# A DiT kernel: seven block products in the first feed-forward too, modulation columns placed anew, and SyncE in program order

## The chip, the core and the metric

The kernel runs on one core of a Trainium2 chip. The metric is the device time of one execution in microseconds. A core has five engines that run their own instruction queues in order: PE (TensorE, matrix multiply, with its weight loads shown as PEld), DVE (VectorE), ACT (ScalarE), POOL (GpSimd) and SP (SyncE, which here issues nearly all loads from HBM). A queue stops at an instruction that waits for another engine's result, for a load, or for a buffer to come free.

## What is computed

A diffusion backbone of two layers on 512 latent tokens of width 1024, with 256 context tokens. Layer 0 mixes by Fourier heads and windowed attention, layer 1 by centred pooling. Each layer ends in a SwiGLU feed-forward with 2816 hidden channels. Every sub-layer has its own shift, scale and gate, which come from the conditioning vector. Cut to what matters here:

```python
def ada_mod(cond, w, b):
    m = jax.nn.silu(cond) @ w + b
    return jnp.split(m[..., None, :], 6, axis=-1)

def modulate(h, shift, scale):
    return h * (1 + scale) + shift

def swiglu(h, w1, w3, w2):
    return (jax.nn.silu(h @ w1) * (h @ w3)) @ w2
```

In each layer the feed-forward adds `gate * swiglu(modulate(rms_norm(h), shift, scale))` to `h`.

## The kernel before

**Layout and precision.** Activations lie with channels on the 128 partitions and the 512 tokens along the free dimension, so `h` is eight tiles of 128 x 512. A product in float32 is made of three passes: each operand is split into a high and a low part, and `passes` (L181 to L185) adds high by high (L183), low weight by high (L184) and high weight by low (L185). ACT makes a weight's high part `w_h` (L68), DVE the low part `w_l` (L153). The class `Stream` (L126) does this for all feed-forward weights: SP loads them into a ring of four raw buffers (`w_r`), ahead of their use.

**Stages.** The modulation of the first sub-layer, the input projections and the attention with its Fourier heads run to about 238 us. Then come layer 0's feed-forward (to 601), the pooling stage (to 638), layer 1's feed-forward (to 981), and the last norm with the stores.

**The feed-forward** (`ffn`, L1018) takes the 22 hidden tiles of 128 channels in groups of 8, 8 and 6 (`GROUPS`). After each group a down projection of eight steps (one for each tile of `h`, index `dt`) adds the group's part to `h` (L1083). Tile 0 is the lead tile (class `Lead`, L301): its product is taken from `h` before the norm's factor is known, and the shift's part, which is `wb` (DVE, L313 and L315) times ones (`sh_ps`, PE, L335), is added afterwards. Meanwhile `norm_apply` (L357) makes the normalized, modulated input of all other tiles: for each of eight channel tiles DVE writes `nrm_u` (L360), ACT `hnh` and DVE `hnl` (L366).

An ordinary tile multiplies two weights of 1024 rows by 512 tokens: 2 x 8 x 3 = 48 matmuls of 512 columns. In layer 1, tiles 4 to 21 (`QUARTERED`, L24) instead run as two by two blocks with seven block products in place of eight (class `Quarters`, L903): 7 x 4 x 3 = 84 matmuls of 256 columns. Sums of blocks of the input (`pieces`, L917: tiles `t_f`, `t_h`, `t_l`) are made once in the ordinary tiles before; sums of blocks of the weights (`prepare`, L944: `s_f`) for each tile. The low parts of the weights that are used as they are come by an accumulating transfer from POOL's queue (`low`, L937 to L942). The sums of blocks need `nrm_u`, so in layer 1 these eight tiles are kept, in the buffers of `a` (L1028, `NA` = 17).

**Modulation columns.** 80 of the columns of 128 modulation values are made one at a time by DVE (class `AdaCols`, L204): SP loads 512 KB into a raw buffer (`ada_r`, L215) and one DVE instruction multiplies by the conditioning vector and sums (L222). 24 are made in the attention (`acol`, over the units of `ADA`, L849: 2 in each of units 0 to 3, 4 in each of units 4 to 7), and 56 (`acol1`) in layer 0's tiles 2 to 21, three per tile (L1071 to L1073). The attention runs in eight such units; their columns are put on DVE in the place where the code stands (`pinned`).

**What sets the order.** In each queue a scheduler places the instructions, except where an engine is in `manual_schedule`, which keeps the order of the code: PE in layer 1's feed-forward. In the last down projection of layer 0, `pool_in` also prepares the pooling stage: it scales each finished tile of `h` (`pxh`, `pxl`, L355) and makes `wsh` (L1117, L1119); the norm adds squares (`sq`, L252).

Of the kernel before, what the change touches and what calls it, by code (L numbers as in the profile page):

```python
# [23 lines left out]
QUARTERED = (frozenset(), frozenset(range(4, NHID)))  # L24
NA = 17
# [6 lines left out]
def kernel(  # L32
# [93 lines left out]
    class Stream:  # L126
# [29 lines left out]
        def slots_for(self, n):  # L156
            pool, t = (wp_, "") if alt["pool"] is None or self.slots % 2 == 0 else (alt["pool"], "2")
            self.slots += 1
            return [pool.tile([P, n], F32R, tag=w + t, bufs=3, name=m) for w, m in (("whi", "w_h"), ("wlo", "w_l"))]

# [43 lines left out]
    class AdaCols:  # L204


        def __init__(self, blocks):
# [9 lines left out]
        def step(self, ahead=1):  # L217
# [4 lines left out]
            nc.vector.scalar_tensor_tensor(out=r, in0=r, scalar=1.0, in1=condB, op0=ALU.mult, op1=ALU.mult,  # L222
                                           accum_out=ada[l][:, t:t + 1])
# [170 lines left out]
    with ExitStack() as es:  # L394
# [507 lines left out]

    class Quarters:  # L903
# [79 lines left out]
        def run(self, left):  # L983
# [34 lines left out]
    def ffn(l, rstd, A, lead, each=None, pool=None):  # L1018
        nonlocal ss
        nrm = Norm(pf, T)  # L1020
# [15 lines left out]
        if quartered:  # L1036
            order.enter_context(tc.manual_schedule(engines={PE}))
        for gi, (j0, nj) in enumerate(GROUPS):
            a = []
            for j in range(j0, j0 + nj):  # L1040
# [269 lines left out]
```

## Time and profile before

| | us |
|---|---|
| median of 3 runs | 997.09 |
| the runs | 999.26, 995.76, 997.09 |
| profiled execution | 996.72 |
| its span, first to last instruction | 995.0 |
| mean granted TensorE clock | 0.994 |

The span is one execution as the hardware profiler recorded it; the profiled execution's own time is 1.7 us longer, as it includes what lies around the span. In the rows below, "L183" is line 183, `h_ps<-hnh,w_h` is the tile written and the tiles read, "x600" a count, and a group's numbers are its busy time in us, the mean of one in ns, and the idle time of the engine ahead of these instructions with what ended it.

```profile
L184 PE MATMUL h_ps<-hnh,w_l 128*128 128x512 f32 (+1 forms) x600 | 210.8, 351 | 0.4 <-DVE w_l L153 0.4
L183 PE MATMUL h_ps<-t_h,w_h 128*128 128x256 f32 x288 | 82.3, 286 | 1.4 <-DVE av L1060 0.9
L1083 DVE SCALAR_TENSOR_TENSOR h<-w_ps,ada,h 128x512 f32<-128x512 f32 x48 | 36.0, 750 | 91.2 <-PE w_ps L185 91.2
```

Matmuls overlap in the pipeline, so the time of one is longer than its share; the distance from one start to the next is what counts.

### The profile page before, as it was taken

Reading aid. Unit: us, or ns where it says so; the run is one execution under the profiler, and the core shown is the slowest. Engines: PE = TensorE matmul, PEld = TensorE weight load, DVE = VectorE, ACT = ScalarE, POOL = GpSimd, SP = SyncE. Lnnn points to the kernel's source line nnn. Section 1 sums busy time; section 2 is a strip of 40 time slices with the busy share of each in tenths; the row PEclk is TensorE's granted clock in tenths of the full one; section 3 lists DMA queues with packets and bytes.
Section 4 is the critical chain, followed back from the end, with each engine's and each line's share of the span. In section 5 each row is a group of like instructions: output and inputs, shape, how many; then the busy total and the mean of one; then the engine's idle time right before and its main releaser. Section 6 shows DMA issues by size and latency. Waiting matters only on the chain.

```text
span 995.0 us, 14007 instructions
## 1 busy us (share of the span) xinstructions
PE 962.3 (97%) x5464; PEld 804.6 (81%) x5464; DVE 665.6 (67%) x1086; ACT 450.6 (45%) x707; POOL 58.5 (6%) x63
## 2 busy tenths in 40 slices
PE   5999999998999999999999999999999999999995
PEld 3767777776888888888888888789988999889984
DVE  4678677879966546655365388998645776458644
ACT  4467666445632212223122365675533765337531
POOL 1011011002000000000000001000010110101100
PEclk9999999999999999999999999999999999999998
DMA  9931211653576546665366333136652786527602
GB/s 338 345 106 32 106 44 65 217 189 119 178 267 239 187 134 219 223 225 193 106 212 200 118 108 127 33 74 181 180 149 64 184 187 176 153 64 174 150 17 85
DMA packets 49602, 153.43 MB, mean 154 GB/s; under 512 B 6016, under 2 KB 6144, under 8 KB 49536
## 3 DMA queue, kind: packets, MB, share of 16 engines
q1 hardware_dynamic: 44352, 138.38, 41.1%
q0 software_dynamic: 5184, 14.16, 8.4%
q8 instruction: 43, 0.70, 0.3%
q14 instruction: 23, 0.19, 0.1%
HBM read 150.41 MB, written 2.10 MB: 153 GB/s over the span
## 4 chain that ended last, share of the span: by engine, by line
PE 89%; DVE 6%; ACT 3%; issue 2%; DMA 0%; DVEq 0%; SPq 0%; ACTq 0%
PE h_ps L183 15%; PE h_ps L184 15%; PE h_ps L185 15%; PE w_ps L184 8%; PE w_ps L183 8%; PE w_ps L185 8%; PE pv_ps L769 2%; PE t_ps L758 2%; PE mo_ps L183 1%; PE mo_ps L185 1%; PE mo_ps L184 1%; ACT w_h L68 1%; PE s_ps L721 1%; PE s_cx L434 1%; DVE w_l L153 1%
## 5 line engine op out<-in xcount | busy, mean ns | idle before, releaser
L68 ACT ACTIVATE w_h<-w_r 128x1024 fp32r<-128x1024 f32 (+2 forms) x158 | 148.7, 943 | 255.1 <-PE h_ps L185 115.8
L184 PE MATMUL h_ps<-hnh,w_l 128*128 128x512 f32 (+1 forms) x600 | 210.8, 351 | 0.4 <-DVE w_l L153 0.4
L183 PE MATMUL h_ps<-hnh,w_h 128*128 128x512 f32 (+1 forms) x600 | 210.9, 351 | 0.0
L185 PE MATMUL h_ps<-hnl,w_h 128*128 128x512 f32 (+1 forms) x600 | 210.7, 351 | 0.0
L153 DVE TENSOR_TENSOR w_l<-w_r,w_h 128x1024 fp32r<-128x1024 f32 (+2 forms) x122 | 137.1, 1126 | 33.6 <-ACT w_h L68 33.2
L222 DVE SCALAR_TENSOR_TENSOR ada_r<-ada_r,condB 128x1024 f32<-128x1024 f32 x80 | 97.6, 1222 | 70.2 <-DMA ada_r<-in_adaR_dram 70.1
L183 PE MATMUL w_ps<-ah,w_h 128*128 128x512 f32 x352 | 137.0, 389 | 0.0
L184 PE MATMUL w_ps<-ah,w_l 128*128 128x512 f32 x352 | 137.0, 389 | 0.0
L185 PE MATMUL w_ps<-al,w_h 128*128 128x512 f32 x352 | 137.0, 389 | 0.0
L184 PEld LDWEIGHTS h_ps<-hnh,w_l 128*128 128x128 f32 x600 | 113.6, 189 | 15.7 <-DVE w_l L153 0.8
L183 PEld LDWEIGHTS h_ps<-hnh,w_h 128*128 128x128 f32 x600 | 113.6, 189 | 15.1
L185 PEld LDWEIGHTS h_ps<-hnl,w_h 128*128 128x128 f32 x600 | 113.6, 189 | 14.9
L1083 DVE SCALAR_TENSOR_TENSOR h<-w_ps,ada,h 128x512 f32<-128x512 f32 x48 | 36.0, 750 | 91.2 <-PE w_ps L185 91.2
L183 PE MATMUL h_ps<-t_h,w_h 128*128 128x256 f32 x288 | 82.3, 286 | 1.4 <-DVE av L1060 0.9
L185 PE MATMUL h_ps<-t_l,w_h 128*128 128x256 f32 x288 | 81.6, 283 | 0.0
L184 PE MATMUL h_ps<-t_h,w_l 128*128 128x256 f32 x288 | 81.5, 283 | 0.0
L185 PEld LDWEIGHTS w_ps<-al,w_h 128*128 128x128 f32 x352 | 66.1, 188 | 13.8
L183 PEld LDWEIGHTS w_ps<-ah,w_h 128*128 128x128 f32 x352 | 66.1, 188 | 13.7
L184 PEld LDWEIGHTS w_ps<-ah,w_l 128*128 128x128 f32 x352 | 66.1, 188 | 13.4
L68 ACT ACTIVATE w_h<-s_f 128x1024 fp32r<-128x1024 f32 x36 | 38.2, 1060 | 60.5 <-PE w_ps L185 30.7
L183 PEld LDWEIGHTS h_ps<-t_h,w_h 128*128 128x128 f32 x288 | 55.2, 192 | 2.6 <-DVE c_q L1004 1.4
L184 PEld LDWEIGHTS h_ps<-t_h,w_l 128*128 128x128 f32 x288 | 55.3, 192 | 0.0
(274 smaller groups left out, 1543.9 us busy)
## 6 DMA issues: line engine op xcount, KB each, us to landing
w_r<-in_w_dram SPq DMA_DIRECT2D x88, 512.0 KB, 4.1
ada_r<-in_adaR_dram SPq DMA_DIRECT2D x80, 512.0 KB, 4.2
w_r<-in_w2a_dram SPq DMA_DIRECT2D x32, 512.0 KB, 4.4
w_l<-in_w_dram POOLq DMA_DIRECT2D x18, 512.0 KB, 5.9
ada_q<-in_adaP_dram SPq DMA_DIRECT2D x32, 256.0 KB, 5.7
w_r<-in_w2b_dram SPq DMA_DIRECT2D x16, 384.0 KB, 3.1
w_l<-in_w_dram POOLq DMA_DIRECT2D x18, 256.0 KB, 6.0
w_r<-in_wo_dram SPq DMA_DIRECT2D x16, 256.0 KB, 2.8
```

Source lines behind the costliest of these rows:

```text
L68: return nc.scalar.activation(out=out, in_=in_, func=func, **kw)
L153: nc.vector.tensor_tensor(lo, src, f32(hi), op=ALU.subtract)
L183: nc.tensor.matmul(acc, wh, mh, start=start, stop=False, skip_group_check=shared)
L184: nc.tensor.matmul(acc, wl, mh, start=False, stop=False, skip_group_check=shared)
L185: nc.tensor.matmul(acc, wh, ml, start=False, stop=stop, skip_group_check=shared)
L222: nc.vector.scalar_tensor_tensor(out=r, in0=r, scalar=1.0, in1=condB, op0=ALU.mult, op1=ALU.mult, accum_out=ada[l][:, t:t + 1])
L434: nc.tensor.matmul(ps[32 * g:32 * g + 32, :], condS[:, kt, :], r[:, k * n:(k + 1) * n], start=(kt < 4), stop=(kt >= 4), tile_position=(0, ...
L721: nc.tensor.matmul(sp[:, c:c + n], q, KH[kv][:, k0:k0 + n], start=True, stop=False)
L758: nc.tensor.transpose(tp[:, c * P:(c + 1) * P], Ps[c][:, n * P:(n + 1) * P], ident)
L769: nc.tensor.matmul(ops[64 * kv:64 * kv + 64, 0:256], VS[:, kbs[n], kv, :], th[:, 256 * kv:256 * kv + 256], start=(n == 0), stop=(n == N - ...
L1083: nc.vector.scalar_tensor_tensor(out=h[:, dt, :], in0=acc, scalar=ada[l][:, 40 + dt:41 + dt], in1=h[:, dt, :], op0=ALU.mult, op1=ALU.add)
```

## The change

1. **Products.** Layer 0's tiles 6 to 21 take the form with seven block products. `nrm_u` of layer 0 is kept for it, in the buffers of `a` in pool `pf` (over the memory that the attention leaves), not in `pb`'s `tmp`. `NA` is 16.
2. **Columns.** 32 columns are made in the attention: 3, 5, 5, 5, 4, 4, 3, 3 in the eight units. Of the other 48, layer 0's feed-forward makes 9 in tiles (2, 3, 4, 5, 9, 11, 13, 17, 19) and 32 in its down projections (13, 13 and 6), and layer 1's tiles 1 to 7 make 7. They have two buffers of their own (`adar` in `pf`) and in the first two down projections two more.
3. **Order.** In both feed-forwards PE and SP keep the order of the code, and the columns stand on DVE where the code puts them.
4. **Memory.** The block sums' pool `pt8` is opened in each `ffn` and closed before the last down projection; only there the pooling stage's `pq` is opened (`pool_stage`). `tmp` in `pf` has 6 buffers.

```diff
-QUARTERED = (frozenset(), frozenset(range(4, NHID)))
-NA = 17
+QUARTERED = (frozenset(range(6, NHID)), frozenset(range(4, NHID)))
+COLUMNS = ((2, 3, 4, 5, 9, 11, 13, 17, 19), (1, 2, 3, 4, 5, 6, 7))
+NA = 16
...
-                self.raw.append(raw_tile(1024, "ada_r"))
+                self.raw.append(self.room[len(self.raw) % len(self.room)]())
...
-            self.load(self.done + ahead)
+            self.load(self.done + self.ahead)
...
-            u = pb.tile([P, n], F32, tag="tmp", bufs=8, name="nrm_u")
+            u = pool.tile([P, n], F32, tag="tmp", bufs=8, name="nrm_u")
...
-        acol = AdaCols([(0, 16), (0, 24), (0, 32)])
+        acol = AdaCols([(0, 8 * k) for k in range(2, 6)])
...
-        ADA, DFT, MIX = (2, 2, 2, 2, 4, 4, 4, 4), (0, 5, 5, 6, 0, 0, 0, 0), (0, 0, 0, 0, 9, 9, 8, 6)
+        ADA, DFT, MIX = (3, 5, 5, 5, 4, 4, 3, 3), (0, 5, 5, 6, 0, 0, 0, 0), (0, 0, 0, 0, 9, 9, 8, 6)
...
-    acol1 = AdaCols([(0, 40)] + [(1, 8 * k) for k in range(6)])
+    def ada_home():
+        return pf.tile([P, 1024], F32, tag="adar", bufs=2, name="ada_r")
+
+    acol1 = AdaCols([(1, 8 * k) for k in range(6)])
+    acol1.room, acol1.ahead = [ada_home], 2
...
-            order.enter_context(tc.manual_schedule(engines={PE}))
+            order.enter_context(tc.manual_schedule(engines={PE, SP}))
...
-                    for _ in range((0, 1, 2, 1)[j]):
+                    for _ in range((0, 1, 2, 1, 0, 0)[j]):
...
-                if l == 0 and j > 1:
-                    for _ in range(3):
-                        acol1.step()
+                if j in COLUMNS[l]:
+                    pinned(DVE, acol1.step)
+            if gi == len(GROUPS) - 1:
+                phase.close()
+                if then:
+                    then()
...
+                if l == 0:
+                    early = gi < 2 and dt < KT - 3
+                    acol1.room = [ada_home] + early * [lambda: pool.tile([P, 1024], F32, tag="s", bufs=2, name="ada_r")]
+                    acol1.ahead = 2 + early
+                    for _ in range(2 if early else gi < 2 or dt < 6):
+                        pinned(DVE, acol1.step)
```

How the instructions move is shown at three places. The first is DVE at the start of layer 0's feed-forward. Before:

```order
L315 SCALAR_TENSOR_TENSOR wb<-w_r,ada_106,wb 128x128 x4
L153 TENSOR_TENSOR w_l<-w_r,w_h 128x1024
L315 SCALAR_TENSOR_TENSOR wb<-w_r,ada_106,wb 128x128
L360 SCALAR_TENSOR_TENSOR nrm_u<-h,Af_2364,bc_ps 128x512
L315 SCALAR_TENSOR_TENSOR wb<-w_r,ada_106,wb 128x128
L360 SCALAR_TENSOR_TENSOR nrm_u<-h,Af_2364,bc_ps 128x512
L315 SCALAR_TENSOR_TENSOR wb<-w_r,ada_106,wb 128x128
L366 SCALAR_TENSOR_TENSOR hnl<-nrm_u,ada_106,hnh 128x512
```

and with the change (lines stand two lower there):

```order
L151 TENSOR_TENSOR w_l<-w_r,w_h 128x1024
L313 SCALAR_TENSOR_TENSOR wb<-w_r,ada_106,wb 128x128 x4
L358 SCALAR_TENSOR_TENSOR nrm_u<-h,Af_2389,bc_ps 128x512
L151 TENSOR_TENSOR w_l<-w_r,w_h 128x1024
L358 SCALAR_TENSOR_TENSOR nrm_u<-h,Af_2389,bc_ps 128x512
L364 SCALAR_TENSOR_TENSOR hnl<-nrm_u,ada_106,hnh 128x512
L358 SCALAR_TENSOR_TENSOR nrm_u<-h,Af_2389,bc_ps 128x512
L364 SCALAR_TENSOR_TENSOR hnl<-nrm_u,ada_106,hnh 128x512
```

All `wb` now stand ahead of the first `nrm_u`; in the new order this `nrm_u` waits for PE's `sh_ps`, which reads `wb`, and the split of tile 1's second weight stands right behind it.

The second place is DVE in the last down projection of layer 0, about its sixth and seventh additions to `h`. Before:

```order
L1083 SCALAR_TENSOR_TENSOR h<-w_ps,ada_106,h 128x512
L315 SCALAR_TENSOR_TENSOR wb<-w_r,ada_107,wb 128x128
L1117 TENSOR_SCALAR wsh<-w_r,ada_107 128x256 x2
L1119 SCALAR_TENSOR_TENSOR wsh<-w_r,ada_107,wsh 128x256
L252 TENSOR_TENSOR sq<-sq 128x512
L355 SCALAR_TENSOR_TENSOR pxl<-h,Am_4910,pxh 128x512
L1119 SCALAR_TENSOR_TENSOR wsh<-w_r,ada_107,wsh 128x256
L153 TENSOR_TENSOR w_l<-w_r,w_h 128x1024
L1083 SCALAR_TENSOR_TENSOR h<-w_ps,ada_106,h 128x512
```

and with the change:

```order
L1089 SCALAR_TENSOR_TENSOR h<-w_ps,ada_106,h 128x512
L220 SCALAR_TENSOR_TENSOR ada_r,ada_107<-ada_r,condB 128x1024
L250 TENSOR_TENSOR sq<-sq 128x512
L353 SCALAR_TENSOR_TENSOR pxl<-h,Am_5964,pxh 128x512
L1133 TENSOR_SCALAR wsh<-w_r,ada_107 128x256 x2
L1135 SCALAR_TENSOR_TENSOR wsh<-w_r,ada_107,wsh 128x256 x2
L151 TENSOR_TENSOR w_l<-w_r,w_h 128x1024
L1089 SCALAR_TENSOR_TENSOR h<-w_ps,ada_106,h 128x512
```

A modulation column (`ada_r`) has come in behind the sixth addition, and the `wb` sums have left for the pooling stage. All four `wsh` stand ahead of the `w_l`.

The third place is DVE in the attention, between the scores of one unit and those of the next: `mx` and `nm` belong to the softmax, `U`, `Ul`, `gl` and `rr` to the Fourier heads, `y_sb` to their result and `o` to the attention's. Before:

```order
L672 TENSOR_TENSOR Ul<-U,Uh 128x514
L222 SCALAR_TENSOR_TENSOR ada_r,ada_106<-ada_r,condB 128x1024
L746 RECIPROCAL r_1404<-s_1402 128x4
L730 TENSOR_SCALAR nm<-mx,nsink 128x1
L729 TENSOR_REDUCE mx<-s_ps 128x1
L681 TENSOR_TENSOR gl<-g_ps,gh 128x512
L730 TENSOR_SCALAR nm<-mx,nsink 128x1
L729 TENSOR_REDUCE mx<-s_ps 128x1
L730 TENSOR_SCALAR nm<-mx,nsink 128x1
L739 TENSOR_TENSOR d_1591<-nm,sink_sb 128x4
L688 TENSOR_TENSOR rr<-e_ps,rr 2x128
L744 TENSOR_TENSOR s_1595<-sm,e_1593 128x4
```

and with the change:

```order
L670 TENSOR_TENSOR Ul<-U,Uh 128x514
L220 SCALAR_TENSOR_TENSOR ada_r,ada_106<-ada_r,condB 128x1024 x2
L728 TENSOR_SCALAR nm<-mx,nsink 128x1
L225 TENSOR_TENSOR ada_106<-ada_106,adaB_sb 128x8
L742 TENSOR_TENSOR s_1415<-sm,e_1413 128x4
L727 TENSOR_REDUCE mx<-s_ps 128x1
L744 RECIPROCAL r_1417<-s_1415 128x4
L728 TENSOR_SCALAR nm<-mx,nsink 128x1
L679 TENSOR_TENSOR gl<-g_ps,gh 128x512
L220 SCALAR_TENSOR_TENSOR ada_r,ada_106<-ada_r,condB 128x1024
L727 TENSOR_REDUCE mx<-s_ps 128x1
L686 TENSOR_TENSOR rr<-e_ps,rr 2x128
```

Where one column stood within twelve rows behind `Ul`, three do now, two of them back to back ahead of the softmax's `nm`, and a fourth follows.

More of the change, by code (lines that the diff above doesn't have):

```diff
@@ L68, in act @@
         return nc.scalar.activation(out=out, in_=in_, func=func, **kw)
-    DVE, ACT, PE = mybir.EngineType.DVE, mybir.EngineType.Activation, mybir.EngineType.PE
+    DVE, ACT, PE, SP = [getattr(mybir.EngineType, e) for e in ("DVE", "Activation", "PE", "SP")]
     def last(engine):
@@ L154, in split @@
             return hi, lo
[L156 to L159, printed above, removed]
         def take(self, n):
@@ L179, in peek, with slots_for @@
             return self.raw[self.used + n]
+        def slots_for(self, n):
+            pool, t = (wp_, "") if alt["pool"] is None or self.slots % 2 == 0 else (alt["pool"], "2")
+            self.slots += 1
+            return [pool.tile([P, n], F32R, tag=w + t, bufs=3, name=m) for w, m in (("whi", "w_h"), ("wlo", "w_l"))]
     def passes(acc, w, m, start, stop, shared=False):
@@ L208, in __init__ @@
             self.tasks = [(l, t) for l, t0 in blocks for t in range(t0, t0 + 8)]
-            self.raw, self.done = [], 0
+            self.raw, self.done, self.ahead, self.room = [], 0, 1, [lambda: raw_tile(1024, "ada_r")]
         def load(self, n):
@@ L987, in run @@
             r = [self.ps.tile([P, 256], F32, tag=f"q{q}", bufs=1, name="h_ps") for q in range(4)]
-            x, y, si = sf("x"), sf("y"), sf("si")
-            c = self.pool.tile([P, 768], F32, tag="c", bufs=1, name="c_q")
-            q0, q1, q2 = [slice(256 * q, 256 * q + 256) for q in range(3)]
+            x, y, si, c = sf("x"), sf("y"), sf("si"), sf("c_q")
+            q0, q1 = slice(0, 256), slice(256, 512)
             self.product(r[0], w["a1"], 0, "b11", start=True)
@@ L1009, in run, with ffn @@
             self.product(r[2], w["s34"], 512, "b22")
-            nc.vector.tensor_tensor(c[:, q0], x[:, q1], r[2], op=ALU.add)
-            act(si[:, q1], c[:, q0], AF.Silu)
+            nc.vector.tensor_tensor(y[:, q1], x[:, q1], r[2], op=ALU.add)
+            act(si[:, q1], y[:, q1], AF.Silu)
             self.product(r[3], w["a22"], 0, "t4")
-            nc.vector.tensor_tensor(c[:, q1], x[:, q1], r[3], op=ALU.add)
+            nc.vector.tensor_tensor(c[:, q0], x[:, q1], r[3], op=ALU.add)
             av = sf("av")
-            nc.vector.tensor_tensor(av, si, c[:, 256:768], op=ALU.mult)
+            nc.vector.tensor_tensor(av, si, c, op=ALU.mult)
             return av
-    def ffn(l, rstd, A, lead, each=None, pool=None):
+    def ffn(l, rstd, A, lead, each=None, then=None):
         nonlocal ss
-        nrm = Norm(pf, T)
+        phase = ExitStack()
+        pool = phase.enter_context(tc.tile_pool(name="pt8", bufs=1, reuse_waits="tile"))
+        nrm = Norm(pf, T, sq=("tmp", 6, "tmp", 6))
         hn, late, us = [], [], []
@@ L1132, in pool_in @@
             pool_shift(kt - 5)
-    nrm = ffn(0, rstd, Af, lead, pool_in)
+    nrm = ffn(0, rstd, Af, lead, pool_in, pool_stage)
     rs_c = nrm.rstd_cols()
@@ L1200 @@
     stage.close()
-    with tc.tile_pool(name="pt8", bufs=1, reuse_waits="tile") as pt8:
-        rstd = ffn(1, rstd, Af1, lead, pool=pt8).rstd_short()
+    rstd = ffn(1, rstd, Af1, lead).rstd_short()
     wide.close()
```

23 lines of the change are left out of this document (12 added, 11 removed).

## The prediction

> **What bounds the kernel now.** I began with the busy table and the chain of waits on the page, then cut the span at its stages, and then asked in each stage what PE (TensorE's matrix multiply) waits for.
>
> ```profile
> PE 962.3 (97%) x5464; PEld 804.6 (81%) x5464; DVE 665.6 (67%) x1086; ACT 450.6 (45%) x707; POOL 58.5 (6%) x63
> PE 89%; DVE 6%; ACT 3%; issue 2%; DMA 0%; DVEq 0%; SPq 0%; ACTq 0%
> ```
>
> PE is busy in 97% of the span and holds 89% of the chain. So fewer PE cycles are worth their full length wherever PE has no gaps, and whatever else the change moves costs only where it makes a gap. The stages say where that is. The columns are: window, its length, busy time (and instructions) of PE, its weight loads, DVE, ACT and POOL, then the granted clock, the DMA share and GB/s. The rows are: attention units 1 to 3; layer 0's first down projection; its tiles 8 to 15; tiles 16 to 21; last down projection; the pooling stage; layer 1's tiles 0 to 3; 4 to 7; 8 to 15; 16 to 21.
>
> ```profile
> 120.00:160.00 40.00, 39.49 (x288) 28.85 (x287) 29.97 (x73) 25.19 (x60) 4.05 (x3) 1.00 0.15 53
> 329.40:372.90 43.50, 43.50 (x194) 36.04 (x193) 20.64 (x24) 10.08 (x11) 0.00 (x0) 1.00 0.44 145
> 372.90:459.90 87.00, 87.00 (x385) 72.08 (x384) 53.18 (x78) 23.38 (x30) 0.00 (x0) 1.00 0.66 221
> 503.50:568.70 65.20, 65.20 (x289) 54.01 (x288) 32.12 (x51) 18.22 (x25) 0.00 (x0) 1.00 0.54 178
> 568.70:601.40 32.70, 32.70 (x147) 27.09 (x145) 29.62 (x56) 19.62 (x28) 0.00 (x0) 1.00 0.37 118
> 601.40:638.50 37.10, 34.31 (x269) 29.69 (x267) 31.90 (x49) 21.68 (x36) 4.76 (x4) 1.00 0.24 77
> 638.50:677.40 38.90, 38.90 (x176) 32.24 (x175) 36.30 (x56) 24.80 (x32) 2.82 (x4) 1.00 0.39 88
> 677.40:719.70 42.30, 41.13 (x338) 40.52 (x337) 31.36 (x47) 25.45 (x37) 3.46 (x4) 1.00 0.62 172
> 763.20:844.90 81.70, 81.43 (x674) 80.88 (x673) 61.33 (x95) 52.43 (x74) 10.44 (x12) 1.00 0.67 164
> 888.40:948.90 60.50, 60.50 (x506) 60.49 (x505) 43.73 (x69) 36.96 (x54) 6.96 (x8) 1.00 0.57 139
> ```
>
> Layer 0's tiles and its down projections have no gap on PE at all. Tiles in the new form (layer 1 from tile 4) have nearly none. DVE is the next engine, and it is already close to full in three places: 29.62 of 32.7, 31.90 of 37.1 and 36.30 of 38.9. These are where I look for the cost.
>
> **The change part by part.**
>
> *A. Products.* Tiles 6 to 21 of layer 0 go from 48 matmuls of 512 columns to 84 of 256. Layer 1 runs the same 84, on the same shapes, so its stages give the price. Tiles 6 and 7 cost 2/8 of 87.00 = 21.75 before, and with the windows of 87.0 and 65.2 that makes 173.95. After, layer 1 gives 42.3/2 = 21.15 for the two tiles in which the form begins, then 81.7 and 60.5: 163.35. **−10.6.** The matmuls themselves allow a little more.
>
> ```profile
> 429.76 0.39 PE L185 MATMUL h_ps<-hnl,w_h 128*128 128x512 f32 x1
> 429.98 0.39 PE L183 MATMUL h_ps<-hnh,w_h 128*128 128x512 f32 x1
> 779.75 0.28 PE L183 MATMUL h_ps<-t_h,w_h 128*128 128x256 f32 x1
> 779.87 0.28 PE L184 MATMUL h_ps<-t_h,w_l 128*128 128x256 f32 x1
> ```
>
> From start to start a matmul of 512 columns takes about 0.227 (87.00/384) and one of 256 takes 0.120, so a tile goes from 10.88 to 10.08, and 16 tiles save 12.8. That is the far end of this term; −10.6 contains layer 1's entry gap. The Trainium skill ("TensorE: Matmul & The Clock Gate", "Back-to-back issue gap") gives for an isolated warm matmul N/2.4 + 2.5 ns. By that a tile would go from 10.35 to 9.17, and the estimate for 16 tiles would be −18.9. The page adds that with weight loads in the stream the spacing is set by both. The trace agrees with that warning: 120 ns against the formula's 109, with the weight loads busy for 80.88 of 81.7. So the rows stand.
>
> What lies beside these products: DVE gets 61.33 plus three columns (tiles 9, 11, 13) in 81.7, and ACT 52.43. Both fit. The columns leave the ordinary tiles, where PE had no gap, so their going gains nothing.
>
> *B. Start of layer 0's feed-forward.* The values `nrm_u` move to memory that the lead product's shift still reads. The new first `nrm_u` must wait until `sh_ps` ends; in before it ran during the lead product.
>
> ```profile
> 245.38 0.74 DVE L360 SCALAR_TENSOR_TENSOR nrm_u<-h,Af,bc_ps 128x512 f32<-128x512 f32 x1
> 252.04 0.50 PE L335 MATMUL sh_ps<-ones,wb 128*128 128x1 f32 x4
> 252.40 0.48 PE L183 MATMUL h_ps<-hnh,w_h 128*128 128x512 f32 x1
> 252.58 0.17 ACT L68 ACTIVATE lb<-sh_ps 128x2 f32<-128x2 f32 x1
> 252.65 0.71 ACT L68 ACTIVATE hnh<-nrm_u,ada 128x512 fp32r<-128x512 f32 x1
> 252.68 1.23 DVE L153 TENSOR_TENSOR w_l<-w_r,w_h 128x1024 fp32r<-128x1024 f32 x1 [0.74 <-ACT w_h L68]
> 257.34 1.06 ACT L68 ACTIVATE w_h<-w_r 128x1024 fp32r<-128x1024 f32 x1 [0.70 <-DMA w_r<-in_w_dram]
> ```
>
> I replay it with these durations. `sh_ps` ends at 252.54 and `nrm_u` at 253.3. On ACT the first `hnh` stands behind `lb` and a `w_h` (1.06), so it ends at 254.5, where PE's tile 1 starts: 2.1 later than 252.40. On DVE the second `w_l` follows the first `nrm_u`, so it starts at 253.2 rather than 252.68, and the weight that is loaded into its place reaches ACT at 257.9 rather than 257.34. That `w_h` now stands on ACT ahead of the last five `hnh`. The first of these ends at 259.7, its `hnl` follows, and five steps of six matmuls remain: 259.7 + 30 × 0.227 = 266.5, with 0.2 for `hnl` 266.7. Before, tile 1 began at 252.40, ran 10.88 and lost 0.4, which gives 263.7. **+3.0**, between the 2.1 of the late start and 5 (the load half a landing later).
>
> *C. Attention.* Units 0 to 3 get 18 columns instead of 8; units 4 to 7 have two fewer. The five in each of units 1 to 3 replace two each: 9 more.
>
> ```profile
> L222 DVE SCALAR_TENSOR_TENSOR ada_r<-ada_r,condB 128x1024 f32<-128x1024 f32 x80 | 97.6, 1222 | 70.2 <-DMA ada_r<-in_adaR_dram 70.1
> 141.06 1.14 DVE ada_r L222 x2
> PE g_ps L183 <- ACT Uh L68: 0.5, 1, 0.5
> ```
>
> 9 × 1.22 = 11.0 of DVE on 29.97 makes 41.0 in a window of 40: 1.0 over. The chain of waits shows a column (141.06) already between a matmul and the one that follows from it, and the waits on PE between 100 and 170 show 0.5 behind it (`g_ps` for `Uh`). With DVE full I expect one such wait in each of three units: 1.0 + 3 × 0.5 = **+2.5**. Below: 0, if neighbouring units take the overflow. Above: 11.4, if all ten added columns stand on the chain like that one (1.14 each).
>
> *D. Last down projection and pooling.* Six columns (7.3) enter. The 16 `wb` sums for layer 1's lead tile (4.9 + 0.6) leave for the pooling stage, because their weights are now loaded behind the column loads in SyncE's program order.
>
> ```profile
> L315 DVE SCALAR_TENSOR_TENSOR wb<-w_r,ada,wb 128x128 f32<-128x128 f32 x14 | 4.9, 349 | 0.2
> L313 DVE TENSOR_SCALAR wb<-w_r,ada 128x128 f32<-128x128 f32 x2 | 0.6, 282 | 0.0
> L153 DVE TENSOR_TENSOR w_l<-w_r,w_h 128x768 fp32r<-128x768 f32 (+1 forms) x8 | 8.7, 1090 | 3.2 <-ACT w_h L68 3.2
> L1119 DVE SCALAR_TENSOR_TENSOR wsh<-w_r,ada,wsh 128x256 f32<-128x256 f32 x4 | 1.8, 480 | 0.0
> L1117 DVE TENSOR_SCALAR wsh<-w_r,ada 128x256 f32<-128x256 f32 x4 | 1.2, 354 | 0.0
> PE pl_ps L1176 <- ACT zh L68: 1.2, 2, 0.8
> PE z_ps L183 <- DVE z L1161: 0.7, 2, 0.4
> ```
>
> In sum 29.62 + 7.3 − 5.5 = 31.4 still fits in 32.7; in order it doesn't. Between the sixth and the seventh addition to `h` DVE now has the addition, a column, `sq`, `pxl`, four `wsh` and a `w_l`: in a chain about 0.66 + 1.14 + 0.60 + 0.66 + 1.7 + 1.14 = 5.9 (queued instructions start about 0.08 before the end of the one ahead, as the timeline of DVE shows), against a step of 32.7/8 = 4.09. The last additions come 1.8 late, and PE's norm and last `z_ps` wait for them. The pooling stage then asks 31.90 + 5.5 = 37.4 of DVE in 37.1, 0.3 more. PE has no cover there, since it already waits on these chains. **+2.1**; from 0 to 4.2 (7.3 less DVE's 3.1 idle in the down projection).
>
> *E. Start of layer 1.* Columns 1 to 3 enter a window with 36.30 of 38.9 used: 3.7 against 2.6 of room, so **+1.1** (0 to 3.7), late at the wait that ends this window.
>
> ```profile
> PE h_ps L183 <- DVE av L1060: 0.9, 1, 0.9
> ```
>
> The other four enter 42.3 with 31.36 used (+4.9) and fit.
>
> *At nothing.* 13 columns in each of layer 0's first two down projections are 15.9 on a DVE with 20.64 of 43.5 used. Their 6.8 MB raise 145 GB/s to about 300, while the page's first slices move more:
>
> ```profile
> GB/s 338 345 106 32 106 44 65 217 189 119 178 267 239 187 134 219 223 225 193 106 212 200 118 108 127 33 74 181 180 149 64 184 187 176 153 64 174 150 17 85
> ```
>
> SyncE in program order lets a column load that waits for its buffer hold up the weight loads behind it; DVE's idle time covers that. Without that cover it costs about one landing:
>
> ```profile
> w_r<-in_w_dram SPq DMA_DIRECT2D x88, 512.0 KB, 4.1
> w_l<-in_w_dram POOLq DMA_DIRECT2D x18, 512.0 KB, 5.9
> 771.98 0.87 POOL L941 DMA_DIRECT2D w_l<-in_w_dram  x1 [16.02 <-ACT w_l L68]
> ```
>
> Sum: −10.6 + 3.0 + 2.5 + 2.1 + 1.1 = −1.9. The profiled execution took 996.72 (span 995.0), so after 994.8; it lies 0.37 below the median of the runs, 997.09, so **995.2** beside that median.
>
> **The rivals.**
>
> *Covers hold (faster).* B is a wait that the order shows, but C, D and E rest on full queues, and instructions may find gaps that I call taken. With B alone and half of D (1.0): −10.6 + 4.0 = −6.6, so 990.5. For it: PE in units 1 to 3 lost only 0.5 of 40. Against it: DVE's load in the three windows. With B at 2.1 and all else at nothing it is 988.6.
>
> *DVE becomes the bound of the attention (slower).* Its place is units 1 to 3, its mechanism the one at 141.06: a column stands in DVE's queue ahead of a softmax or Fourier step for which PE waits. At 1.14 each, ten cost 11.4: −10.6 + 11.4 + 3.0 + 2.1 + 1.1 = +7.0, or 1004.1. It passes slower by 0.3% when C exceeds 7.4, that is from seven of the ten on the path. For it: DVE has 41.0 to do in 40. Against it: in before PE lost 0.5 there, although the path ran over a column.
>
> *Seven products are slower in layer 0 than in layer 1 (the change doesn't do what it says).* The lows of some of these weights come by a POOL transfer (5.9 to land, 0.87 to issue). In layer 1 PE lost 0.27 in 81.7 with DVE at 75%; here DVE stands at (61.33 + 3.7)/81.7 = 80%. If each of 16 tiles waited a microsecond for its transfer, the saving would be gone: about 1011. Little speaks for it. The Trainium skill ("SBUF — State Buffer", "Who interferes with whom") says that such transfers starve while DVE runs copies or `tensor_scalar` in a two-port mode, and that `tensor_tensor` has no such mode. Here the splits are `tensor_tensor`, and POOL's 0.87 in layer 1 shows no stall.
>
> **How the numbers follow.** Forecast 0.45, covers hold 0.34, attention 0.18, slow products 0.03. A measurement here can tell about 0.3% (3 us) from no change. The forecast's own spread puts 0.05 of its 0.45 below that bound; of covers hold 0.31 is faster; of the attention rival 0.17 is slower. So faster 0.36, same 0.44, slower 0.20. The range: down to **989.5**, covers hold nearly whole; up to **1001.5**, the sum with C at 6 and D at its upper 4.2 (−10.6 + 3.0 + 6 + 4.2 + 1.1 = +3.7, 1000.8) and some more. The attention rival's upper half and the slow products stay outside.
>
> **What would show each step.** A: layer 0's tiles 8 to 15 take near 81.7 with no PE wait. B: PE's first `h_ps` of tile 1 follows `sh_ps` by about 2, waiting for ACT's `hnh`, and tile 1 ends some 3 late. C: the stretch from the first unit to the end of the fourth grows by about 2.5, with PE waits for `Uh`, `p` or other results of DVE. D: the last addition to `h` follows the last `w_ps` by nearly 2, and the stage to the lead product of layer 1 is longer by 2. E: layer 1's tiles 0 to 3 grow by 1. The forecast is wrong if the attention keeps its length (then towards 992), or if PE waits for weights in layer 0's tiles (then SyncE's order or POOL's transfers were the cost I put at nothing).

## The result, and the profile after

The changed kernel took 1008.63 us in the median of four runs (1006.95 to 1012.66), the kernel before 997.65 beside it. The ratio is 1.0118, with a 95% interval from 1.0099 to 1.0136: about 11 us **slower**, outside the range of the prediction and on its other side. The profiled execution took 1008.31, its span is 1006.5 and its mean clock 0.991.

The page after, the busy table's first row and the chain of waits by engine:

```profile
PE 955.5 (95%) x6040; PEld 823.5 (82%) x6040; DVE 739.3 (73%) x1251; ACT 510.2 (51%) x807; POOL 86.3 (9%) x95
PE 56%; DVE 19%; DMA 12%; ACT 6%; issue 5%; SPq 1%; DVEq 0%; ACTq 0%
```

PE has 7 us less to do, and yet the span is 11.5 longer. DMA and SyncE's queue (SPq) hold 13% of the chain, where they held none.

The same views by stage, in the order: layer 0's tiles 8 to 15, its tiles 16 to 21, the pooling stage, layer 1's tiles 0 to 3, its tiles 4 to 7 (columns as in the prediction).

```profile
379.20:463.50 84.30, 82.23 (x674) 81.13 (x673) 68.47 (x109) 50.69 (x76) 11.31 (x13) 1.00 0.71 193
507.10:571.00 63.90, 61.95 (x506) 60.83 (x505) 50.84 (x84) 36.53 (x56) 7.83 (x9) 1.00 0.69 183
603.60:641.80 38.20, 33.91 (x260) 28.59 (x259) 36.65 (x71) 22.43 (x36) 3.85 (x3) 1.00 0.21 68
642.60:681.80 39.20, 39.20 (x178) 32.49 (x177) 37.35 (x58) 22.89 (x30) 1.77 (x2) 1.00 0.33 104
681.80:730.00 48.20, 41.48 (x338) 40.61 (x337) 37.54 (x60) 28.32 (x41) 5.22 (x6) 1.00 0.81 228
```

To compare whole executions I cut every trace at the starts of PE's matmuls, from the first of one stage to the first of the next. Each column is one profiled execution. "Attention" runs from the first norm to the end of the norm before the lead product; "start" is the lead product's rest with tiles 1 to 5; the products are tiles 6 to 21 without the down projections between them; the sum is up to the start of the last matmul.

| us | before | after | difference | predicted |
|---|---|---|---|---|
| attention (C) | 232.39 | 234.18 | +1.8 | +2.5 |
| layer 0's start (B) | 64.15 | 67.78 | +3.6 | +3.0 |
| layer 0's products (A) | 174.08 | 170.10 | −4.0 | −10.6 |
| last down projection, pooling (D) | 68.91 | 70.87 | +2.0 | +2.1 |
| layer 1, tiles 1 to 3 (E) | 32.78 | 32.78 | 0 | +1.1 |
| layer 1, tiles 4 to 7 | 42.29 | 48.19 | +5.9 | 0 |
| all other | 371.13 | 373.42 | +2.3 | 0 |
| sum | 985.73 | 997.32 | +11.6 | −1.9 |

Two rows are far off: the products won 6.6 us too little, and layer 1's tiles 4 to 7, whose products did not change, lost 5.9. Here is what PE waits for in the latter stage, from the list of waits (sum, times, longest); `y` is a sum of block products, `av` the tile's finished product, and both are made by DVE:

```profile
PE h_ps L181 <- DVE y L1001: 2.9, 2, 2.7
PE h_ps L181 <- DVE av L1063: 2.7, 1, 2.7
PE h_ps L181 <- ACT x L69: 1.1, 1, 1.1
```

PE waits mostly for DVE, so DVE's load looks like the cause. The timeline says what DVE waits for, with the chain's piece from a weight's load to `av` (lines are up to two lower than before, until the feed-forward's code):

```profile
673.85 1.22 DVE L220 SCALAR_TENSOR_TENSOR ada_r<-ada_r,condB 128x1024 f32<-128x1024 f32 x1
675.10 0.33 SPq L213 DMA_DIRECT2D ada_r<-in_adaR_dram  x1
675.52 1.20 SPq L135 DMA_DIRECT2D w_r<-in_w_dram  x2
675.64 0.42 ACT w_l L69
676.06 8.50 DMA w_r<-in_w_dram
684.66 0.69 DVE L954 TENSOR_TENSOR s_f<-w_r 128x512 f32<-128x512 f32 x1 [1.41 <-DMA w_r<-in_w_dram]
685.26 0.68 DVE L1063 TENSOR_TENSOR av<-si,h_ps 128x512 f32<-128x512 f32 x1
```

It is a loop. DVE finishes a column at about 675.0; that frees a buffer, so SyncE issues the next column's load at 675.10, and only then, at 675.52, the weights that stand behind it. They reach DVE at 684.66. DVE's sum of blocks waits for them, and behind it in DVE's queue stands `av`, for which PE waits. This piece alone does not tell what the column's load costs: the second of the two weight loads, the one that `s_f` reads, was released at 676.06 by ACT's work on an earlier weight, half a microsecond behind the first. In layer 0's tiles 8 to 15 the order is plain. SyncE waits 13 to 20 us for each column's buffer, and then four weights follow at once:

```profile
406.15 0.33 SPq L213 DMA_DIRECT2D ada_r<-in_adaR_dram  x1
406.58 2.60 SPq L135 DMA_DIRECT2D w_r<-in_w_dram  x4
426.94 0.33 SPq L213 DMA_DIRECT2D ada_r<-in_adaR_dram  x1
427.36 2.12 SPq L135 DMA_DIRECT2D w_r<-in_w_dram  x4
```

SyncE's list of waits has grown in the same way; before, then after:

```profile
SPq L215 <- DVE ada_r L222: 89.8, 34, 7.5
SPq L213 <- DVE ada_r L220: 247.2, 50, 22.0
```

### The profile page after: what moved, and what is told of

Read it like the earlier page. It is cut to its first block, busy times and chain, and to the rows that moved or that the text cites. A ratio compares the mean times of both kernels' runs of the same rounds, so it can differ in the third digit from the quotient of the medians.

```text
span 1006.5 us, 15502 instructions
## 1 busy us (share of the span) xinstructions
PE 955.5 (95%) x6040; PEld 823.5 (82%) x6040; DVE 739.3 (73%) x1251; ACT 510.2 (51%) x807; POOL 86.3 (9%) x95
## 4 chain that ended last, share of the span: by engine, by line
PE 56%; DVE 19%; DMA 12%; ACT 6%; issue 5%; SPq 1%; DVEq 0%; ACTq 0%
DMA w_r<-in_w_dram 8%; PE h_ps L181 7%; PE h_ps L183 7%; PE h_ps L182 7%; PE w_ps L183 6%; PE w_ps L181 6%; PE w_ps L182 6%; DVE w_l L151 4%; ACT w_h L69 3%; DVE ada_r L220 3%; PE pv_ps L767 2%; DMA w_r<-in_w2a_dram 2%; PE mo_ps L181 1%; PE t_ps L756 1%; DMA ada_q<-in_adaP_dram 1%
## 5 line engine op out<-in xcount | busy, mean ns | idle before, releaser
L69 ACT ACTIVATE w_h<-w_r 128x1024 fp32r<-128x1024 f32 (+2 forms) x158 | 141.5, 898 | 185.0 <-DMA w_r<-in_w_dram 52.6
L181 PE MATMUL h_ps<-hnh,w_h 128*128 128x256 f32 (+1 forms) x536 | 167.6, 313 | 8.5 <-DVE y L1001 5.4
L183 PE MATMUL h_ps<-hnl,w_h 128*128 128x256 f32 (+1 forms) x536 | 166.2, 310 | 0.8 <-DVE hnl L364 0.8
L182 PE MATMUL h_ps<-hnh,w_l 128*128 128x256 f32 (+1 forms) x536 | 165.9, 309 | 0.0
L181 PE MATMUL h_ps<-t_h,w_h 128*128 128x256 f32 x544 | 155.4, 286 | 5.8 <-DVE av L1063 3.3
L182 PE MATMUL h_ps<-t_h,w_l 128*128 128x256 f32 x544 | 154.1, 283 | 0.0
L183 PE MATMUL h_ps<-t_l,w_h 128*128 128x256 f32 x544 | 154.0, 283 | 0.0
L181 PEld LDWEIGHTS h_ps<-t_h,w_h 128*128 128x128 f32 x544 | 104.4, 192 | 7.9 <-DVE c_q L1005 4.1
L943 POOL DMA_DIRECT2D w_l<-in_w_dram x68 | 59.3, 872 | 569.4 <-ACT w_l L69 392.8
L183 PEld LDWEIGHTS h_ps<-t_l,w_h 128*128 128x128 f32 x544 | 104.4, 192 | 0.0
L151 DVE TENSOR_TENSOR w_l<-s_f,w_h 128x1024 fp32r<-128x1024 f32 x68 | 83.1, 1224 | 17.2 <-ACT w_h L69 16.4
```

Source lines behind the costliest of these rows:

```text
L69: return nc.scalar.activation(out=out, in_=in_, func=func, **kw)
L151: nc.vector.tensor_tensor(lo, src, f32(hi), op=ALU.subtract)
L181: nc.tensor.matmul(acc, wh, mh, start=start, stop=False, skip_group_check=shared)
L182: nc.tensor.matmul(acc, wl, mh, start=False, stop=False, skip_group_check=shared)
L183: nc.tensor.matmul(acc, wh, ml, start=False, stop=stop, skip_group_check=shared)
L943: nc.gpsimd.dma_start(out=lo, in_=dram, accum_op=ALU.add)
```

## The experiments

**Theory 1**: in program order a column load that waits for its buffer stands at the head of SyncE's queue and holds up weight loads. **Theory 2**: DVE simply has too much to do. The start (B) and the attention (C) are tested beside them. The table at the end of this section has the stages of every run.

*Column loads one ahead, and SyncE's queue given back to the scheduler.* The first edit:

```diff
-    acol1.room, acol1.ahead = [ada_home], 2
+    acol1.room, acol1.ahead = [ada_home], 1
...
-                    acol1.ahead = 2 + early
+                    acol1.ahead = 1 + 2 * early
```

> The column loads into the two home buffers are issued one column ahead instead of two, so that SyncE never has to wait for the column that DVE is only about to make. Nothing else changes. Theory 1 (in SyncE's program order a column load that waits for its buffer holds up the weight loads behind it, and PE then waits for the sums that DVE makes of late weights): layer 0's tiles 8 to 15 fall from 84.3 us to about 81.7 and 16 to 21 from 63.9 to about 61, layer 1's tiles 4 to 7 from 48.2 to about 42.5, SyncE's waits for columns nearly vanish; 8 to 12 us less than the changed kernel, about 997 to 1000. Theory 2 (DVE has too much to do there, whenever the weights come): PE still waits for sums of DVE in these tiles, less than 3 us are won.

Ratio to before 1.0046 (1.0024 to 1.0068). The runs spread from 997.33 to 1005.47. Some 7 us of the 11.8 are won: tiles 16 to 21 are at 60.6, layer 1's tiles 4 to 7 at 45.7, but tiles 8 to 15 stay at 84.35. SyncE still waits 196.4 us for columns in all, over half of it in the down projections; in tiles 8 to 15 its waits for column buffers fall from 70.2 to 8.8 us. So these waits no longer explain that stage. About 1.8 of the 2.8 us that it is longer than in the next run arise in its first tile, where DVE waits 1.73 us, until 387.02, for weights that SyncE asked for only from 377.70 on; before that SyncE had waited for DVE's `s_f` to free their buffers, and `s_f` stood behind the down projection's addition and column. The rest was not followed up.

The second edit:

```diff
-            order.enter_context(tc.manual_schedule(engines={PE, SP}))
+            order.enter_context(tc.manual_schedule(engines={PE}))
```

> SyncE's queue is again ordered by the scheduler in both feed-forwards; column loads are still asked for two ahead. Theory 1 (a waiting column load at the head of SyncE's queue holds up weights): the gain depends on where the scheduler puts the column loads; if it puts them behind weights that are needed earlier, layer 1's tiles 4 to 7 fall from 48.2 to under 45, and 4 us or more are won in all; where it leaves them ahead, the loss stays in that stage, and the SyncE waits for columns stand there. Theory 2 (DVE's load): unchanged within 2 us in every stage.

Ratio 1.0017 (1.0001 to 1.0034), about 10 us less than the changed kernel. Its rows for layer 0's tiles 8 to 15 and 16 to 21:

```profile
382.60:464.10 81.50, 81.23 (x673) 80.75 (x672) 68.36 (x109) 52.17 (x75) 10.43 (x12) 1.00 0.83 222
507.60:568.30 60.70, 60.70 (x506) 60.58 (x505) 49.66 (x81) 36.99 (x56) 6.96 (x8) 1.00 0.73 194
```

These are the stages of the prediction's term A, to 0.2 us, with the same DVE work (68.4 for 68.5) and the same loads. So neither DVE's time nor the loads' traffic had cost the nearly 6 us there (170.1 less 164.4): it was the order of SyncE's loads.

*The two theories taken apart.* One run keeps the 48 columns' work on DVE and drops their loads, the other keeps the loads and drops most of the work:

```diff
-                nc.sync.dma_start(out=self.raw[-1], in_=adaR[48 * l + t])
+                if self.loads:
+                    nc.sync.dma_start(out=self.raw[-1], in_=adaR[48 * l + t])
...
-            nc.vector.scalar_tensor_tensor(out=r, in0=r, scalar=1.0, in1=condB,
+            nc.vector.scalar_tensor_tensor(out=r, in0=r if self.loads else condB, scalar=1.0, in1=condB,
```

> The 48 columns that the feed-forwards make keep their place and their work on DVE, but read a vector that is on the chip, so SyncE issues no load for them; their sums are then not the modulation (layer 1's shift, scale and gate are left out). Theory 1 (SyncE's queue: column loads that wait hold up weight loads): the waits for weights go; layer 0's tiles 8 to 15 take about 81.7, 16 to 21 about 60.6, layer 1's tiles 4 to 7 about 42.5 to 44, 8 us or more are won. Theory 2 (DVE has too much to do): these stages stay within 1 us of the changed kernel's 84.3, 63.9 and 48.2.

```diff
-            nc.vector.scalar_tensor_tensor(out=r, in0=r, scalar=1.0, in1=condB, op0=ALU.mult, op1=ALU.mult,
+            n = 1024 if self.ahead == 1 else 64
+            nc.vector.scalar_tensor_tensor(out=r[:, :n], in0=r[:, :n], scalar=1.0, in1=condB[:, :n], op0=ALU.mult, op1=ALU.mult,
```

> The same 48 columns keep their loads, their buffers and their place, but DVE multiplies and sums 64 of the 1024 elements (about 0.15 us instead of 1.22), so the modulation is only a part of the sum. Theory 1 (SyncE waits until DVE reaches a column's place in its queue, and the weights stand behind): most of the loss stays, less than 5 us are won, and SyncE's waits for columns stay over 150 us in sum. Theory 2 (the time that the columns take on DVE): 8 us or more are won.

Without loads: 0.9991 (0.9971 to 1.0011), 12 to 13 us less than the changed kernel. With short columns: 1.0090 (1.0064 to 1.0116), about 3 us less, an interval that overlaps the changed kernel's. The first's rows for layer 0's tiles 8 to 15, 16 to 21 and layer 1's tiles 4 to 7, and the second's SyncE waits:

```profile
382.90:465.10 82.20, 81.54 (x674) 80.86 (x673) 68.32 (x109) 52.45 (x75) 10.42 (x12) 1.00 0.74 182
508.70:569.20 60.50, 60.50 (x506) 60.43 (x505) 49.56 (x81) 36.95 (x56) 6.96 (x8) 1.00 0.65 167
677.90:721.80 43.90, 41.38 (x338) 40.57 (x337) 38.25 (x60) 26.62 (x39) 4.35 (x5) 1.00 0.68 180
SPq L213 <- DVE ada_r L221: 316.0, 43, 21.1
```

DVE is as busy as in the changed kernel in layer 1's tiles 4 to 7 (38.25 for 37.54), and the stage takes 43.9 instead of 48.2. Taking four fifths of the columns' time away (0.22 us each instead of 1.22) leaves tiles 8 to 15 at 86.2. **Theory 1 holds, theory 2 falls.**

*The start.* Two runs. The first only lets the pool that takes over the attention's memory wait tile by tile:

```diff
-    pf = ctx.enter_context(tc.tile_pool(name="pf", bufs=2))
+    pf = ctx.enter_context(tc.tile_pool(name="pf", bufs=2, reuse_waits="tile"))
```

> The pool that takes over the attention's memory waits for each tile that lies there, not for the last use of the whole memory. Theory (the first nrm_u of layer 0 waits for the lead product's shift through this memory): PE's tile 1 starts right behind the shift, and tile 1 ends 3 to 4 us earlier; 3 to 4 us less than the changed kernel, about 1005. Rival (the start is late because of DVE's order of weight splits and wb sums alone): tile 1 still starts 2 us after the shift, less than 1 us is won.

Ratio 1.0123 (1.0096 to 1.0151): nothing won. `nrm_u` now began during the lead product, but PE's tile 1 still waited 1.8 us. In the changed kernel the place reads as follows (DVE, then ACT three times, then PE):

```profile
254.68 0.75 DVE L358 SCALAR_TENSOR_TENSOR nrm_u<-h,Af,bc_ps 128x512 f32<-128x512 f32 x1 [7.24 <-PE sh_ps L333]
253.61 1.06 ACT L69 ACTIVATE w_h<-w_r 128x1024 fp32r<-128x1024 f32 x1 [9.88 <-PE h_ps L183]
254.67 1.06 ACT L69 ACTIVATE w_h<-w_r 128x1024 fp32r<-128x1024 f32 x1
255.64 0.71 ACT L69 ACTIVATE hnh<-nrm_u,ada 128x512 fp32r<-128x512 f32 x1
256.39 0.50 PE L181 MATMUL h_ps<-hnh,w_h 128*128 128x512 f32 x1 [1.83 <-ACT hnh L69]
```

With DVE's wait gone, ACT's remained: the splits of the next weights stand ahead of `hnh` and wait for the lead product. The second run adds an order on ACT: five `hnh`, then the split of tile 1's second weight, the others and `lb` behind the sixth.

```diff
+            if l == 0 and kt == 5:
+                ws.LS = 0
+                with tc.issue_after(last(ACT)):
+                    early = ws.get(), ws.get()
+                ws.LS = 2
+                split = last(DVE)
...
+                if j == 0 and l == 0:
+                    with tc.issue_after(sixth):
+                        av = lead.result(rstd, sf)
...
+                    with tc.issue_after(sixth) if l == 0 else ExitStack():
+                        wA, wB = early if l == 0 and j == 1 else (ws.get(), ws.get())
```

> Layer 0's start: the pool that takes over the attention's memory waits tile by tile, and ACT's queue is pinned so that five hnh stand ahead of the split of tile 1's second weight, and lb behind them. Theory (the late start is two waits behind each other: nrm_u for the shift's memory on DVE, and in ACT's queue a weight split ahead of hnh that waits for the lead product): tile 1 starts within 0.5 us of the shift instead of 2.0, the granted clock stays at 1.00 from 252 to 265, and the stretch from the lead's last norm step to the end of tile 5 is 3 to 4 us shorter. Rival (DVE cannot make eight nrm_u and hnl in time anyway): less than 1.5 us are won.

Ratio 1.0087 (1.0061 to 1.0112), 3.1 us less than the changed kernel; the intervals overlap, so it is the stage that shows the gain. Tile 1 starts right behind the shift, and the stage takes 64.6 instead of 67.8, nearly as before (64.15):

```profile
255.76 0.50 PE L333 MATMUL sh_ps<-ones,wb 128*128 128x1 f32 x4
256.12 0.48 PE L181 MATMUL h_ps<-hnh,w_h 128*128 128x512 f32 x1
```

*The attention.* The 32 columns put as 2, 2, 2, 2, 6, 6, 6, 6:

> Units 0 to 3 of the attention make two columns each, as before the change, and units 4 to 7 six each; still 32 in all. Theory (columns in DVE's queue ahead of softmax results delay PE in units 1 to 3): the stretch from the first norm to the output projection is 1 to 2 us shorter, PE's wait for o (2.5 us) goes; if six columns are then late in units 4 to 7, the gain is given back there. Rival (the attention's added time comes from the column loads, not their place): unchanged within 0.5 us.

Ratio 1.0153 (1.0130 to 1.0175), 3.5 us more than the changed kernel, with intervals that just overlap. The part up to the output projection is 1.9 us shorter, as foreseen, and PE's wait of 2.5 us for DVE's `o` is gone; but the output projection with its norm is 5.1 longer: the price comes later. Layer 1's tiles 4 to 7 took 52.6 in this trace and 51.9 in the run with the pool by tile, with the same code as the changed kernel there (48.2): what this stage loses varies by some 4 us from one execution to another.

*Repairs together.* SyncE scheduled, loads one ahead, the start ordered, and layer 1's seven columns moved to layer 0:

```diff
-COLUMNS = ((2, 3, 4, 5, 9, 11, 13, 17, 19), (1, 2, 3, 4, 5, 6, 7))
+COLUMNS = ((2, 3, 4, 5, 7, 9, 11, 13, 17, 19), ())
...
-                    for _ in range(2 if early else gi < 2 or dt < 6):
+                    for _ in range(2 if gi < 2 else dt < 6):
```

> Three repairs together: SyncE's queue ordered by the scheduler with column loads asked for one ahead, the start of layer 0's feed-forward ordered as in the earlier run on it, and no columns in layer 1's tiles (six of the seven go to the first two down projections of layer 0, one to its tile 7). If the losses are the waits behind column loads and the two waits at the start, and if they add up: layer 0's tiles 8 to 15 about 81.6, 16 to 21 about 60.6, layer 1's tiles 4 to 7 about 42.4, lead to tile 5 about 64.5; 14 to 16 us less than the changed kernel, 992 to 995, so faster than before by 0.2 to 0.5%. If the DVE time of the moved columns matters: the stages with more columns grow, and the sum is not under 997.

> The same three repairs, and the attention again makes 24 columns, in the places that it had before the change; the other eight go to layer 0's tiles (18 there in all). If the attention's extra columns cost what the changed kernel's attention shows over before (1.8 us from the first norm to the lead, or up to 4 with the lower clock that follows): 2 to 4 us less than the run with three repairs alone. If nine columns in tiles 8 to 15 and 16 to 21 cost more in DVE time than that: not faster than that run, with PE waiting for sums of DVE in those tiles.

Both gave 1.0004 (0.9995 to 1.0014, and 0.9994 to 1.0013): all of the loss undone, nothing won. The first had been expected at 992 to 995, but its tiles 8 to 15 took 82.9, 16 to 21 62.0 and layer 1's tiles 4 to 7 46.0, for 81.6, 60.6 and 42.4. With loads asked for one ahead, DVE waits 1.98 us for a column's own load at 506.67, and PE 1.03 for DVE's `y` at 511.70; the rest was not followed up. With the attention as before that part is 2.0 shorter, but layer 0's products give 2.0 back: here the columns were moved, not hidden. In the first the granted clock is low twice about the start. PE there, behind a wait of 1.3 us:

```profile
255.95 0.51 PE L182 MATMUL h_ps<-hnh,w_l 128*128 128x512 f32 x1 [1.34 <-DVE w_l L151]
256.29 0.49 PE L183 MATMUL h_ps<-hnl,w_h 128*128 128x512 f32 x1
256.58 0.63 PE L181 MATMUL h_ps<-hnh,w_h 128*128 128x512 f32 x1
257.00 0.63 PE L182 MATMUL h_ps<-hnh,w_l 128*128 128x512 f32 x1
```

Matmuls of 512 columns start 0.42 apart rather than 0.23 for some three us. The last run closes this gap and the one at the norm:

```diff
-        nrm = Norm(pt, T, eng=nc.gpsimd, direct=2)
+        nrm = Norm(pt, T, eng=nc.gpsimd, direct=3)
...
-            if l == 0 and kt == 5:
+            if l == 0 and kt == 4:
```

> The run with three repairs, and two gaps of PE at the start of layer 0's feed-forward closed: the norm ahead of the lead product adds one square less on POOL (PE waited 0.5 us for it, and the granted clock was 0.86 in the ten us behind), and the split of tile 1's second weight stands one hnh earlier (PE waited 1.3 us for it, clock 0.83 behind). If these short gaps cost more than themselves because PE runs slower for some us behind them: the granted clock stays at 1.00 from 230 to 260, the output projection with the lead is about 2 us shorter and tiles 1 to 5 about 2.5; 992 to 994, faster than before by 0.3 to 0.5%. If the gaps cost only their own 1.8 us: about 995.5, and the clock still falls. If the third square on PE takes the place of POOL's sum as the last to come: no gain at the norm.

Ratio **0.9959 (0.9942 to 0.9975)**, 992.67 us in the median: 4 us less than before, and this version beats both kernels. The windows from 240 to 260, with three repairs and then with the gaps closed:

```profile
240.00:250.00 10.00, 10.00 (x49) 7.50 (x48) 9.33 (x20) 3.59 (x6) 0.00 (x0) 0.86 0.46 134
250.00:260.00 10.00, 8.66 (x33) 6.64 (x32) 9.58 (x17) 5.81 (x9) 0.00 (x0) 0.83 0.55 181
240.00:250.00 10.00, 8.48 (x60) 6.32 (x52) 9.89 (x21) 4.00 (x8) 0.00 (x0) 1.00 0.23 80
250.00:260.00 10.00, 10.00 (x47) 8.21 (x46) 8.92 (x14) 6.19 (x10) 0.00 (x0) 1.00 0.66 235
```

The clock stays at 1.00. The norm and projection are 1.6 us shorter (75.63 to 74.02) and the start 3.0 (66.30 to 63.26), for gaps of 0.5 and 1.3.

All runs by stage, as in the first table (attention, start, products, last down and pooling, layer 1's tiles 4 to 7, sum to the start of the last matmul). Each row is one execution, not the median: that of "one ahead" is 3.7 us below its median, those of "SyncE scheduled" and "gaps closed" 2.0 and 2.2 above theirs.

| us | C | B | A | D | tiles 4–7 | sum |
|---|---|---|---|---|---|---|
| before | 232.4 | 64.2 | 174.1 | 68.9 | 42.3 | 985.7 |
| changed | 234.2 | 67.8 | 170.1 | 70.9 | 48.2 | 997.3 |
| one ahead | 233.8 | 69.0 | 167.1 | 68.6 | 45.7 | 989.2 |
| SyncE scheduled | 236.8 | 68.9 | 164.4 | 69.9 | 46.4 | 990.7 |
| pool by tile | 234.3 | 67.2 | 169.6 | 70.4 | 51.9 | 999.4 |
| columns 2 and 6 | 237.3 | 67.5 | 170.1 | 70.1 | 52.6 | 1002.5 |
| no loads | 237.4 | 68.6 | 164.9 | 70.3 | 43.9 | 988.3 |
| short columns | 234.1 | 67.8 | 170.6 | 68.4 | 49.6 | 996.2 |
| start ordered | 236.8 | 64.6 | 168.7 | 69.8 | 49.1 | 993.8 |
| three repairs | 233.8 | 66.3 | 167.0 | 70.0 | 46.0 | 986.3 |
| attention as before | 231.7 | 66.7 | 169.0 | 70.0 | 47.3 | 988.4 |
| gaps closed | 234.7 | 63.3 | 166.4 | 70.5 | 45.7 | 983.5 |

## Why the prediction was wrong

**The step that failed** is the one that stood under "at nothing": "SyncE in program order lets a column load that waits for its buffer hold up the weight loads behind it; DVE's idle time covers that." The mechanism was named and its cover was wrong. I looked at DVE's share (61 of 82) and not at when it reaches a column: with two buffers and loads asked for two ahead, a load waits for the very column that DVE makes next, 13 to 20 us in layer 0's tiles 8 to 15, and the weights behind it are asked for only then, however idle DVE is. Nor is the price one landing of 4.1 us, once: it comes back in several tiles, 5.7 us in layer 0's products (170.1 against 164.4 with SyncE scheduled) and 4.3 in layer 1's tiles 4 to 7 (48.2 against 43.9 without loads). The prediction's own list said that a wait for weights in layer 0's tiles would mean this cost; it gave it no chance of its own.

**A** was right as a price of the products: without the loop, tiles 6 to 21 take 164.4 (scheduled) and 164.9 (no loads), 9.7 and 9.2 less than before, for the 10.6 of the sum. What was lost was not in the products themselves, so the rival of slower products falls as well.

**B** was right in size (+3.6 for +3.0, taken back by the ordering run), but only partly in mechanism. The wait through the memory is there, yet ACT's queue alone kept tile 1 late when that wait was gone. And the sum had no place for a slower clock: behind the gap 0.75 was granted from 256 to 260 and 0.82 from 260 to 264.

**C** came to +1.8 for +2.5, and here the traces need care. Some executions, that of before among them, have a low clock from 80 to 90 us (0.83) and the changed kernel's has not; the attention of one and the same code takes 236.8 to 237.4 with it and 233.8 to 234.3 without. So the table compares an execution with the low clock to one without it, and that its +1.8 lies near the forecast is partly luck. Among executions without the low clock the attention costs 2.1 to 2.6 more than with its columns as before (231.7), and here the mechanism is the forecast one: between 100 and 215 us PE waits 2.5 us for DVE's `o`, and this wait is gone in both runs that put two columns back in units 0 to 3. Among executions with the low clock the attention costs 4.4 to 5.0 more than before. Half of that is the gap at the norm with its slow clock, since the last run, which closes the gap, stands at 234.7. The attention rival (+11.4) didn't happen.

**D** was right in size (+2.0 for +2.1) and in its first step: the last addition to `h` starts 2.4 us behind the start of the last `w_ps` matmul (605.77, 603.35), where before it was 0.5 (601.64, 601.12). Which part of it is the column and which the moved `wb` was not tried apart. **E** was wrong: layer 1's first tiles, where I found DVE over-full, lost nothing, and the next four, which "fit", lost 5.9. Fullness of an engine told nothing here. Of these 5.9 the column loads hold 4.3 (no loads: 43.9). In the runs without columns in layer 1 the stage still takes 45.7 to 47.3; there PE waits 2.9 to 3.2 us for `av` at the entry (0.9 before), and in the trace with three repairs tile 4's second block of weights reaches ACT 22.1 us after tile 1 begins, where before it was 16.5. Why it lands later was not settled.

## What to carry to other kernels

An instruction queue that issues loads in program order runs only as far ahead as its slowest buffer: before a queue is put into program order, list each load that waits for a buffer, who frees it and when, and what stands behind. Loads of a secondary stream with few buffers belong behind the loads that the critical engine needs next, or the queue stays with the scheduler. And a stage's busy share bounds what fits, not what is on time: the wait was found by following the queue that issues, not the engine that is busy.

## What the runs showed of the hardware

A short gap on PE can cost more than itself. At the norm before the lead product PE was busy 2.29 of 4 us before and 1.78 after, with 0.5 more of waiting; in the next 4 us the granted clock was 1.00 before and 0.62 after. The windows before, then after, then PE's rows after, 512 columns each:

```profile
236.00:240.00 4.00, 2.29 (x24) 1.28 (x23) 4.00 (x6) 2.43 (x4) 0.60 (x1) 1.00 0.01 4
240.00:244.00 4.00, 3.93 (x27) 2.85 (x26) 4.00 (x12) 1.74 (x4) 0.00 (x0) 1.00 0.00 0
236.00:240.00 4.00, 1.78 (x21) 0.86 (x20) 4.00 (x6) 2.44 (x5) 1.29 (x1) 1.00 0.00 0
240.00:244.00 4.00, 4.00 (x18) 2.50 (x19) 3.90 (x11) 2.61 (x5) 0.00 (x0) 0.62 0.13 16
240.64 0.40 PE L181 MATMUL h_ps<-hA,w_h 128*128 128x512 f32 x1
240.87 0.55 PE L182 MATMUL h_ps<-hA,w_l 128*128 128x512 f32 x1
241.22 0.63 PE L183 MATMUL h_ps<-hA,w_h 128*128 128x512 f32 x1
241.65 0.63 PE L181 MATMUL h_ps<-hA,w_h 128*128 128x512 f32 x1
242.08 0.63 PE L182 MATMUL h_ps<-hA,w_l 128*128 128x512 f32 x1
```

The start distance goes from 0.23 to 0.43 for about 3 us. Closing gaps of 1.8 us in sum won 4.6 in these stages.

The Trainium skill ("TensorE: Matmul & The Clock Gate", "What's actually happening") says that the clock halves after an idle window of about 3.4 us, in windows that run freely. The halving agrees with the rows, but here waits of 0.5 to 1.3 us, beside others near them (1.7 us at the norm), were enough to reach it.

They do not always reach it. In the run with the start ordered PE waits the same 1.34 us for the same `w_l` as in the run with three repairs, and the matmuls behind it keep their distance of 0.23:

```profile
258.64 0.50 PE L182 MATMUL h_ps<-hnh,w_l 128*128 128x512 f32 x1 [1.34 <-DVE w_l L151]
258.97 0.39 PE L183 MATMUL h_ps<-hnl,w_h 128*128 128x512 f32 x1
259.20 0.39 PE L181 MATMUL h_ps<-hnh,w_h 128*128 128x512 f32 x1
```

The granted clock there is 1.00 from 256 to 264, where with three repairs it is 0.57 from 256 to 260. The start takes 64.6 us in the one and 66.3 in the other. What decides between the two was not tried.
